# Half of the pooled features behind the attention's first scores, and products of the identity with itself at four changes of stage

## The chip, the cores and the metric

The kernel runs on one core of a Trainium2 chip. The time of a run is the device time of that core in microseconds (us), from the start of the program to its end. A core has five engines with a queue of instructions each, worked off in order and tied to one another by semaphores: TensorE (PE in the rows, its weight loads PEld), VectorE (DVE), ScalarE (ACT), GpSimd (POOL) and SyncE (SP), which here issues most DMA transfers. TensorE's results go to PSUM banks, which VectorE or ScalarE must read before the next product of that bank.

## The reference, cut to what matters

Two blocks on 256 rows of 1024 features, in float32. The first block is one layer with three groups of dilated window attention and a pooling branch; the second is two layers with modulated LayerNorms, a mixer (scans in layer 0, window attention in layer 1) and a squared-ReLU MLP of width 4096. Layer 0 works on the 256 latent rows and 256 context rows, layer 1 needs of the context only keys and values.

```python
# first block
h = rmsnorm(x, norm_g[l]) * (1.0 + scale) + shift
qkv, z_attn, u_pool, z_pool, g_attn, g_pool = split(h @ w_in[l])
# per group: o = softmax(q k^T + bias) v over a dilated band; merged over groups by log-sum-exp
y_attn = (attn * silu(z_attn)) @ w_attn_br[l]
pooled = multiscale_pool(u_pool)            # trailing means over 2, 4, 8, 16 rows, minus the row
y_pool = ((pooled @ pool_w[l]) * pool_scale[l] * silu(z_pool)) @ w_pool_br[l]
x = x + gate * ((sigmoid(g_attn) * y_attn + sigmoid(g_pool) * y_pool) @ w_out[l])
# second block, layer i (xc: the context's rows)
h = x * (1 + sc1) + sh1;  hc = xc * (1 + csc1) + csh1
y = mixer(h, hc) @ w_out                    # i = 1: window attention over latent and context keys
x = layer_norm(alpha * x + g1 * y)
x = layer_norm(alpha * x + g2 * (square(relu((x * (1 + sc2) + sh2) @ w1)) @ w2))
# i = 0: the same two residual steps for xc
```

## The kernel before, in words

**Products.** Every large product is made of three TensorE matmuls of fp32r operands (`mm3`, lines 159 to 161): each operand is split into a rounded high part and a remainder, and hi·hi, hi·lo and lo·hi are added up in one PSUM bank. Weights arrive by DMA in tiles of 512 KB (`raw`), and ScalarE (line 135, `whi`) and VectorE (line 136, `wlo`) split them. `gemm_a` puts features on the partitions, `gemm_b` rows. The banks of products have the name `mm`; `S` holds scores, `T` transposes, `O` smaller results.

**Order.** The program is written as one Python program, and a scheduler puts its instructions on each engine in an order that it works out along a timeline of its own. `tc.issue_after(x)` forces what is issued in its scope behind the instruction x. `queued[...]` keeps the last instruction of a kind. On the chip each engine then keeps that order: an instruction that waits holds back all that stand behind it on its engine.

**First block.** After q, k, v and `z_attn` the 512 pooled features `u` are computed by two `gemm_a` of 256 features, 48 matmuls each (lines 583 and 584); GpSimd forms their trailing sums and VectorE subtracts (lines 587 to 598). The attention follows (function `attention`): for each half of the heads and each tile of 128 queries, scores on TensorE (line 630), softmax on VectorE and ScalarE (line 642), transposes of the result (`pr`, and `xs`, via line 195), products with v (line 654). Between these, `fill(n)` takes steps from a list of fillers, which form the conditioning vectors of the second block: DMA of a tile of `w_mod` (`mvraw`), its products with the condition on TensorE (line 245, two matmuls of 512 columns for each tile), and sums on VectorE (line 288). Behind the first softmax stands `fill(3)`.

**Second block.** `modulate` takes one tile of 128 normalised rows (T = 0 and 1 are the context's, 2 and 3 the latent's): two groups of four transposes into a bank `T` (line 195), ScalarE scales and shifts each 128x128 square (line 342, `hf`), VectorE splits the result into high part and remainder (lines 345 and 346, `hBh`, `hBl` in layer 0's MLP, `hCh`, `hCl` for layer 1's projection, `hDh`, `hDl` for layer 1's MLP; `hBh0b` and the like are second halves). What precedes it for a tile is a LayerNorm: two `bn_stats` (line 360), aggregation, an inverse square root on GpSimd (line 200) and the normalising pass on VectorE (line 374).

- Layer 0's MLP begins with the products of `up(0)` (banks `os_`).
- The keys and values of layer 1 begin at `kb_`: the loop takes the latent half first (`half` = 1: keys by `col_part`, values by `gemm_b`, then `modulate` of context tile T = 1 and the queries of the first pair of heads), then the context half. At the end of layer 0 the tiles are normalised in the order 2, 3, 0, 1; in the program text the `modulate` of tile 0 is the last ahead of `kb_`, and that of tile 1 stands in the loop. The latent half needs only tiles 2 and 3.
- `window(kv, c, qt)` makes the scores of the window attention (line 1289), from `Q`, half of which is moved to other partitions by a DMA (`qr`), and from `KK`.
- Layer 1's MLP begins with `up(0)` in its own form: for i = 0 and 1 a `gemm_b` of 24 matmuls on latent tile 2 + i, ReLU and square on ScalarE (lines 1067 and 1068), four transposes of `f`, and a split.

Of the kernel before, what the change touches and what calls it, by code (L numbers as in the profile page):

```python
# [10 lines left out]
F32 = mybir.dt.float32  # L11
# [84 lines left out]
def body(tc, a, cst, out):  # L96
    nc = tc.nc
    with ExitStack() as ctx:
# [7 lines left out]
        def bank(tag):  # L106
            return psum.tile([P, 512], F32, tag=tag, name=tag, bufs={"mm": 3, "S": 2, "T": 2, "O": 1}[tag])
# [49 lines left out]
        def mm3(o, lhs, rhs, first, last):  # L157
            (lh, ll), (rh, rl) = lhs, rhs
            nc.tensor.matmul(o, lh, rh, start=first, stop=False)  # L159
            nc.tensor.matmul(o, lh, rl, start=False, stop=False)  # L160
            queued["mm"] = nc.tensor.matmul(o, ll, rh, start=False, stop=last).ins  # L161

        def col_part(o, ws, j, xs_):

# [11 lines left out]
        def gemm_b(ws, xh, xl, t):  # L176

            n = ws[0][0].shape[-1]
            o = bank("mm")[:, :n]
            for k, w in enumerate(ws):  # L180
                mm3(o, (xh[:, k, t * P:(t + 1) * P], xl[:, k, t * P:(t + 1) * P]), w, k == 0, k == len(ws) - 1)
            return o
# [10 lines left out]

        def transpose(o, i, n=P):
            return nc.tensor.transpose(o, i, ident[:n, :n])  # L195

        def rsqrt(v, n):

# [131 lines left out]
            nc.vector.tensor_add(B, B, sh[:, :, vec])  # L330
            return A, B

        def modulate(z, cols, dst, t0):

            A, B = cols
            for c in range(0, KC, 4):
                pt = bank("T")
                hf = tmp([P, 4, P], "hf")
                for i in range(4):
                    transpose(pt[:, i * P:(i + 1) * P], z[:, (c + i) * P:(c + i + 1) * P])  # L340
                for i in range(4):
                    queued["hf"] = nc.scalar.activation(hf[:, i, :], pt[:, i * P:(i + 1) * P], AF.Identity, scale=A[:, c + i:c + i + 1],  # L342
                                                        bias=B[:, c + i:c + i + 1]).ins
                hi, lo = (t[:, c:c + 4, t0:t0 + P] for t in dst)
                nc.vector.tensor_copy(hi, hf)
                queued["mod"] = nc.vector.tensor_sub(lo, hf, hi.bitcast(F32)).ins  # L346
# [232 lines left out]
        for i in range(2):  # L579
            silu2(za[:, 2 * i:2 * i + 2, :], gemm_a(w_in, 4608 + 256 * i, xk))  # L580


        for i in range(2):
            nc.scalar.copy(u[:, 2 * i:2 * i + 2, :], gemm_a(w_in, 5120 + 256 * i, xk))
        nc.gpsimd.dma_start(pw, a["pool_w"][0].rearrange("g c e -> c g e"))
        nc.gpsimd.dma_start(icnt, cst["icnt"])
        prev = u
        for s in range(4):
            w_ = 1 << s
            cur = wsum if s == 3 else p1t.tile([P, 4, S], F32, tag="sq", name="wtmp")  # L590
            nc.gpsimd.tensor_add(cur[:, s:, w_:], prev[:, s:, w_:], prev[:, s:, :S - w_])
            nc.gpsimd.tensor_copy(cur[:, s:, :w_], prev[:, s:, :w_])
            if s < 3:
                nc.gpsimd.tensor_copy(wsum[:, s, :], cur[:, s, :])
            prev = cur
        nc.gpsimd.tensor_mul(wsum[:, :, 0:16], wsum[:, :, 0:16], icnt)
        for g in range(4):
            nc.vector.scalar_tensor_tensor(wsum[:, g, :], wsum[:, g, :], 0.5 ** (g + 1), u[:, g, :], op0=ALU.mult, op1=ALU.subtract)

        spare = xs.rearrange("p t n -> p (t n)")  # L600
        yab = slot("h0b", "yab", [P, 2, 4, S], F32R)
# [3 lines left out]
            fill(1)  # L605
        fillers.append(quadcols("b", 2 * D, rows="b0"))
        fillers.append(quadcols("sc2", 4 * D, D // 4))

        def attention(h2):
            Bs = []  # L610
# [5 lines left out]
            for qt in range(2):  # L616
# [8 lines left out]
                for g0, g1 in parts:  # L625
# [5 lines left out]
                    for e in range(2):  # L631
# [1 line left out]
                        nc.vector.tensor_tensor_reduce(out=prs[e][:, g0:g1, 0:nk], in0=sv[e], in1=Bs[e][:, g0:g1, 256 - nk:256], scale=-1.0,  # L633
                                                       scalar=3.0e38 if mins[e] is None else mins[e], op0=ALU.add, op1=ALU.min, accum_out=m)
                        mins[e] = m
                fill(3)
                for e in range(2):
                    pv = prs[e][:, :, 0:nk]
                    den = small.tile([P, 1], F32, tag="den", name="den")
# [411 lines left out]
        def mlp(layer, Ts, xks, y, pool, mid, late, norm, after):  # L1051
# [4 lines left out]
            def up(g):  # L1056

                if g == 3:
                    rate[0] = 3
                fx = (main, pool)[g % 2].tile([P, 8, n], F32R, tag=("qkb", "fx")[g % 2], name="fx")  # L1060
                fh, fl = fx[:, 0:4], fx[:, 4:8]
                if layer and g < 1:
                    ws = w_b(w1, 512 * g)
                    for i in range(2):
                        o = gemm_b(ws, *h2, i)
                        f = pool.tile([P, 512], F32, tag="f", name="f", bufs=2)
                        nc.scalar.activation(f, o, AF.Relu)
                        nc.scalar.activation(f, f, AF.Square)
                        pt = bank("T")
                        for c in range(4):  # L1070
                            transpose(pt[:, c * P:c * P + P], f[:, c * P:c * P + P])
                        tv = pt.rearrange("p (c n) -> p c n", c=4)
                        split(fh[:, :, i * P:i * P + P], fl[:, :, i * P:i * P + P], tv)
                os_ = [bank("mm" if i < 2 else "S")[:, :n] for i in range(4)] if not layer and g == 0 else None
                if not layer and g == 0:
                    ws = [w_a(w1, 256 * i) for i in range(2)]
                    for part, xk_ in xks[0]:
                        for i in range(2):
                            for j in range(2):
                                col_part(os_[2 * i + j][:, part], ws[i], j, xk_)  # L1080
                            mid()
                for i in range(0 if layer and g < 1 else 2):
                    if g:
                        ws = w_a(w1, 512 * g + 256 * i)
                    for j in range(2):
                        if g:
                            o = bank("mm")[:, :n]
                            col_part(o, ws, j, xks[1])
                        else:
                            o = os_[2 * i + j]  # L1090
                        f = pool.tile([P, n], F32, tag="f", name="f", bufs=2)
                        nc.scalar.activation(f, o, AF.Relu)  # L1092
                        nc.scalar.activation(f, f, AF.Square)
                        split(fh[:, 2 * i + j, :], fl[:, 2 * i + j, :], f)
                with tc.issue_after(queued["split"]):
                    late(g)
                if g == 0:
                    rate[0] = 2
                return fh, fl
# [63 lines left out]
        cc = mod_cols("c0b", 2, 6, m0["sc2"], m0["b"][:, 8:16], 1)  # L1163
        cx = mod_cols("x0b", 2, 6, m0["sc2"], m0["b"][:, 8:16], 0)
        h1 = new_h("hB")
        mod0 = lambda T: modulate(r0[:, T, :], (cc, cx)[T // 2], h1, P * T)
        proj_out(r0, a["ev_w_out_2"][0], yH, yL, range(4), mod0)
        lg.close()

# [89 lines left out]
        kT = gc.rearrange("p (j n) -> p j n", j=2)  # L1259
        vN = p4.tile([P, 4, 256], F32, tag="vN", name="vN")  # L1260
        wk, wv = w_a(wq, 1024), w_a(wq, 1280)
        kb_ = [bank("mm"), bank("mm")]
        KK = slot("A0", "KK", [P, 2, 2, 2, 512], F32R)
        for half, xk_ in ((1, hx), (0, hc)):
            hs = slice(S * half, S * half + S)
# [17 lines left out]
        def window(kv, c, qt):  # L1283

            qs = slice(P * qt, P * qt + P)
            sp = [bank("S"), bank("S")]
            for e in range(2):
                for part in range(2):
                    queued["qk"] = nc.tensor.matmul(sp[e], Q2[:, kv % 2, e, c % 2, qs], KK[:, part, kv // 2, kv % 2, :], start=part == 0, stop=part == 1).ins  # L1289
# [109 lines left out]
```

## Time and profile before

| | |
|---|---|
| three runs | 1313.48, 1318.32 and 1324.63 us, median 1318.32 us |
| profiled execution | 1323.18 us, of which the span of the engines' work 1321.4 us |
| TensorE busy | 1272.4 us, 96% of the span, 7777 instructions |
| VectorE, ScalarE, GpSimd busy | 869.6 us (66%), 590.6 us (45%), 85.6 us (6%) |
| mean granted TensorE clock | 0.981 of full speed |
| DMA | 223.80 MB, mean 169 GB/s |

In the rows further down each instruction or group is written as start, duration (us), engine, line, operation, output and inputs, stationary and moving shape for matmuls, and a count; a bracket tells how long the engine had stood idle before it and what ended that. TensorE overlaps neighbouring matmuls, so a matmul's price is the distance from its start to the next one's start and not its duration. The granted clock is 1.00 at 2.4 GHz and 0.50 at 1.2 GHz. A float32 matmul (not fp32r) leaves two records.

### The profile page before, as it was taken

The page shows a single profiled execution, that of the slowest core. Times are in us where ns is not written, and L with a number is a line of the kernel's source. Part 1 is how long each engine was busy: PE and PEld are TensorE (multiplying, and loading weights), DVE is VectorE, ACT ScalarE, POOL GpSimd, SP SyncE. Part 2 cuts the span into 40 slices and gives each one's busy share as a digit, 9 for nine tenths or more (in the row PEclk, how much of TensorE's full clock was granted, in tenths as well). Part 3 has the DMA queues.
Part 4 walks back from the last instruction along what each step waited for, and adds up shares of the span by engine and source line. Part 5 has one row for each costly group of instructions (what it writes and reads, how often), then busy time and mean ns, then how long its engine had stood idle before and what let it go on. Part 6 is the DMA issues. An engine that isn't in the chain of part 4 may idle for free. (4 is left out here: it accounts for less than half of the span.)

```text
span 1321.4 us, 19813 instructions
## 1 busy us (share of the span) xinstructions
PE 1272.4 (96%) x7777; PEld 1045.9 (79%) x7777; DVE 869.6 (66%) x1344; ACT 590.6 (45%) x957; POOL 85.6 (6%) x148
## 2 busy tenths in 40 slices
PE   6999999999999999998999999999998899999996
PEld 5889845998887777778777777777888776788894
DVE  3568844696643357675868876677597677566567
ACT  4434534445431453326334333323445796655660
POOL 2010031000102100001010000000010000000000
PEclk9999969999999999998999999999999999999998
DMA  9789877675441412325656556664345214465651
GB/s 326 263 299 346 271 221 228 206 235 160 148 127 31 127 40 65 128 67 168 201 174 204 163 190 207 207 207 160 96 137 163 71 55 155 150 190 180 187 178 46
DMA packets 140964, 223.80 MB, mean 169 GB/s; under 512 B 8748, under 2 KB 88796, under 8 KB 140870
## 3 DMA queue, kind: packets, MB, share of 16 engines
q1 hardware_dynamic: 134832, 207.64, 49.2%
q0 software_dynamic: 5296, 14.33, 3.6%
q8 instruction: 61, 1.00, 0.3%
q10 hardware_dynamic: 742, 0.55, 0.1%
q14 instruction: 33, 0.27, 0.1%
HBM read 218.23 MB, written 1.12 MB: 166 GB/s over the span
## 5 line engine op out<-in xcount | busy, mean ns | idle before, releaser
L135 ACT CAST whi<-raw 128x1024 fp32r<-128x1024 f32 x261 | 272.9, 1051 | 372.8 <-PE mm L161 203.5
L136 DVE TENSOR_TENSOR wlo<-raw,whi 128x1024 fp32r<-128x1024 f32 x261 | 317.4, 1222 | 162.4 <-ACT whi L135 160.0
L159 PE MATMUL mm<-whi,fx 128*128 128x512 f32 x384 | 153.2, 399 | 2.6 <-DVE y L1112 1.2
L160 PE MATMUL mm<-wlo,fx 128*128 128x512 f32 x384 | 151.4, 395 | 0.0
L161 PE MATMUL mm<-whi,fx 128*128 128x512 f32 x384 | 147.4, 396 | 0.0
L288 DVE SCALAR_TENSOR_TENSOR mva<-mvraw,cst_m,mva 128x1024 f32<-128x1024 f32 x98 | 123.3, 1280 | 0.2
L160 PE MATMUL mm<-A1a,whi 128*128 128x256 f32 x352 | 99.8, 284 | 0.0
L159 PE MATMUL mm<-A1a,whi 128*128 128x256 f32 x352 | 99.8, 283 | 0.0
L161 PE MATMUL mm<-A1a,wlo 128*128 128x256 f32 x352 | 99.6, 283 | 0.0
L160 PE MATMUL mm<-hBl,whi 128*128 128x512 f32 (+1 forms) x256 | 98.4, 384 | 0.1
L159 PEld LDWEIGHTS mm<-whi,fx 128*128 128x128 f32 x384 | 72.2, 188 | 25.1 <-DVE y L1112 6.0
L161 PEld LDWEIGHTS mm<-whi,fx 128*128 128x128 f32 x384 | 72.2, 188 | 17.6 <-DVE fx L111 0.4
L160 PEld LDWEIGHTS mm<-wlo,fx 128*128 128x128 f32 x384 | 72.3, 188 | 16.0
L160 PEld LDWEIGHTS mm<-A1a,whi 128*128 128x128 f32 x352 | 66.2, 188 | 2.4 <-issue 2.3
L111 DVE TENSOR_TENSOR fx<-f,fx 128x512 fp32r<-128x512 f32 (+1 forms) x60 | 34.0, 566 | 51.5 <-ACT fx L110 51.3
L159 PEld LDWEIGHTS mm<-A1a,whi 128*128 128x128 f32 x352 | 66.4, 189 | 1.2 <-issue 1.0
L161 PEld LDWEIGHTS mm<-A1a,wlo 128*128 128x128 f32 x352 | 66.3, 188 | 0.8 <-issue 0.8
L1112 DVE TENSOR_TENSOR y<-y,mm 128x512 f32<-128x512 f32 x72 | 47.1, 683 | 28.2 <-PE mm L161 28.1
L160 PE MATMUL mm<-hDl,whi 128*128 128x256 f32 x224 | 63.1, 282 | 0.0
L1092 ACT ACTIVATE f<-mm 128x512 f32<-128x512 f32 (+1 forms) x58 | 28.4, 490 | 73.0 <-PE mm L161 73.0
L160 PEld LDWEIGHTS mm<-hBl,whi 128*128 128x128 f32 x256 | 48.8, 191 | 10.7 <-DVE hBl L346 0.4
L159 PE MATMUL mm<-whi,hA 128*128 128x512 f32 x128 | 51.2, 401 | 0.0
(519 smaller groups left out, 2846.2 us busy)
## 6 DMA issues: line engine op xcount, KB each, us to landing
raw<-in_mlp_w_dram SPq DMA_DIRECT2D x128, 512.0 KB, 4.1
mvraw<-in_w_mod_dram SPq DMA_DIRECT2D x96, 512.0 KB, 4.7
raw<-in_w_in_dram SPq DMA_DIRECT2D x64, 512.0 KB, 5.4
raw<-in_ev_w_in_dram SPq DMA_DIRECT2D x25, 512.0 KB, 3.9
raw<-in_od_w_qkv_dram SPq DMA_DIRECT2D x12, 512.0 KB, 3.5
mvraw<-in_w_ada_dram SPq DMA_DIRECT2D x10, 512.0 KB, 6.4
raw<-in_w_out_dram SPq DMA_DIRECT2D x8, 512.0 KB, 4.7
raw<-in_ev_w_out_dram SPq DMA_DIRECT2D x8, 512.0 KB, 4.4
```

The source lines that it names most:

```text
L111: queued["split"] = nc.vector.tensor_sub(lo, src, hi.bitcast(F32)).ins
L135: nc.scalar.copy(hi, raw)
L136: queued["lo"] = nc.vector.tensor_sub(lo, raw, hi.bitcast(F32)).ins
L159: nc.tensor.matmul(o, lh, rh, start=first, stop=False)
L160: nc.tensor.matmul(o, lh, rl, start=False, stop=False)
L161: queued["mm"] = nc.tensor.matmul(o, ll, rh, start=False, stop=last).ins
L288: nc.vector.scalar_tensor_tensor(acc, raw, stat[:, k, m:m + 1], acc, op0=ALU.mult, op1=ALU.add)
L1092: nc.scalar.activation(f, o, AF.Relu)
L1112: nc.vector.tensor_add(y[:, T, hs], y[:, T, hs], o)
```

## The change

Two things are changed.

1. In the first block only the first 256 pooled features are computed ahead of the attention. For the other 256 the weights are loaded and split there (`wu`), but the 48 matmuls, the copy to `u` and the whole pooling stand in a new function `pooling`, which is called behind the first softmax of the attention, in place of the `fill(3)` there. That call's three filler steps come later.
2. A helper `awake(n, o, behind)` issues n float32 matmuls of the 128x128 identity with itself into the bank o, forced behind an instruction. Nobody reads these results; the bank's own first product overwrites them. There are 28: 6 and 3 in `modulate` of tile 2 for layer 0's MLP (ahead of each group of four transposes), 2 at layer 0's `up(0)`, 5 at `kb_`, 8 ahead of the first window scores, and 4 at layer 1's `up(0)`. The 2, the 5 and the 4 go through a list `ahead`, and `mm_bank` issues them into the next `mm` bank that is taken, behind `queued["last"]`: the last matmul of a product, or the last transpose of a `modulate`, whichever the program text has put there last.

```diff
-            queued["mm"] = nc.tensor.matmul(o, ll, rh, start=False, stop=last).ins
+            queued["mm"] = queued["last"] = nc.tensor.matmul(o, ll, rh, start=False, stop=last).ins
...
+        ahead = []
+        def awake(n, o, behind):
+            with tc.issue_after(behind):
+                for _ in range(n):
+                    w = nc.tensor.matmul(o[:, :P], ident, ident, start=True, stop=True).ins
+            return w
+        def mm_bank():
+            o = bank("mm")
+            if ahead:
+                awake(ahead.pop(0), o, queued["last"])
+            return o
...
-        def modulate(z, cols, dst, t0):
+        def modulate(z, cols, dst, t0, keep=(0, 0)):
...
+                if keep[c // 4]:
+                    with tc.issue_after(queued["T"]):
+                        queued["awake"] = awake(keep[c // 4], bank("S"), queued["last"])
                 for i in range(4):
-                    transpose(pt[:, i * P:(i + 1) * P], z[:, (c + i) * P:(c + i + 1) * P])
+                    with tc.issue_after(queued["awake"]) if keep[c // 4] else nullcontext():
+                        queued["T"] = queued["last"] = transpose(pt[:, i * P:(i + 1) * P], z[:, (c + i) * P:(c + i + 1) * P]).ins
...
-        for i in range(2):
-            nc.scalar.copy(u[:, 2 * i:2 * i + 2, :], gemm_a(w_in, 5120 + 256 * i, xk))
-        nc.gpsimd.dma_start(pw, a["pool_w"][0].rearrange("g c e -> c g e"))
...
+        nc.scalar.copy(u[:, 0:2, :], gemm_a(w_in, 5120, xk))
+        wu = w_a(w_in, 5376)
...
+        def pooling():
+            o = bank("mm").rearrange("p (j n) -> p j n", j=2)
+            for j in range(2):
+                col_part(o[:, j, :], wu, j, xk)
+            nc.scalar.copy(u[:, 2:4, :], o)
+            nc.gpsimd.dma_start(pw, a["pool_w"][0].rearrange("g c e -> c g e"))
...
-                fill(3)
+                if (h2, qt) == (0, 0):
+                    pooling()
+                else:
+                    fill(3)
...
                 if layer and g < 1:
+                    ahead.append(4)
                     ws = w_b(w1, 512 * g)
...
-                os_ = [bank("mm" if i < 2 else "S")[:, :n] for i in range(4)] if not layer and g == 0 else None
+                if not layer and g == 0:
+                    ahead.append(2)
+                    os_ = [(mm_bank() if i < 2 else bank("S"))[:, :n] for i in range(4)]
...
-        mod0 = lambda T: modulate(r0[:, T, :], (cc, cx)[T // 2], h1, P * T)
+        mod0 = lambda T: modulate(r0[:, T, :], (cc, cx)[T // 2], h1, P * T, (6, 3) if T == 2 else (0, 0))
...
-        kb_ = [bank("mm"), bank("mm")]
+        ahead.append(5)
+        kb_ = [mm_bank(), mm_bank()]
...
+            if (kv, c, qt) == (0, 0, 0):
+                awake(8, sp[0], queued["last"])
```

The scheduler puts the program in order again, so instructions without a line in the diff move too. Three places follow; the line numbers of the changed kernel are up to 35 higher.

TensorE at the end of layer 0's MLP and the start of layer 1's projection, before: `fx` products are the last ones of the MLP, `y` is the tile to be transposed (the four transposes here are the second group of latent tile 3), and `hCh` products are those of the keys and values. The eight transposes of context tile 0 stand some 95 rows further on.

```order
L161 MATMUL mm<-whi,fx 128x512
L195 MATMUL T<-ident,y_5688 128x128 x4
L159 MATMUL mm<-hCh_8358,whi 128x256 x2
L159 MATMUL mm<-whi,hCh_8358 128x256
L160 MATMUL mm<-wlo,hCh_8358 128x256
```

The same place in the changed kernel:

```order
L161 MATMUL mm<-whi,fx 128x512
L195 MATMUL T<-ident,y_5699 128x128 x12
L203 MATMUL mm<-ident 128x128 x5
L159 MATMUL mm<-hCh_8371,whi 128x256
L160 MATMUL mm<-hCl,whi 128x256
```

The twelve transposes are the four from before and the eight of context tile 0, which now stand ahead of every product of the keys and values, with the five products of the identity (line 203) between.

TensorE at the start of layer 1's MLP, before: `aHL` products are the last of the output projection, `r` is the tile to be transposed, `hDh` products are those of `up(0)`. Behind these rows stand 24 such products in all, and then the eight transposes of latent tile 3.

```order
L195 MATMUL T<-ident,r_9841 128x128 x8
L159 MATMUL mm<-whi,aHL 128x512
L160 MATMUL mm<-wlo,aHL 128x512
L161 MATMUL mm<-whi,aHL 128x512 x2
L159 MATMUL mm<-whi,hDh_9847 128x512
L160 MATMUL mm<-wlo,hDh_9847 128x512
L161 MATMUL mm<-whi,hDl 128x512
```

The same place in the changed kernel:

```order
L195 MATMUL T<-ident,r_9867 128x128 x8
L159 MATMUL mm<-whi,aHL 128x512
L160 MATMUL mm<-wlo,aHL 128x512
L161 MATMUL mm<-whi,aHL 128x512 x2
L195 MATMUL T<-ident,r_9867 128x128 x8
L203 MATMUL mm<-ident 128x128 x4
L159 MATMUL mm<-whi,hDh_9873 128x512
L160 MATMUL mm<-wlo,hDh_9873 128x512
```

The eight transposes of tile 3 have moved ahead of the products of tile 2, with the four products of the identity; 48 `hDh` and `hDl` products follow without a break.

TensorE at the start of the attention, before: the 48 products of the second half of `u` come first, then scores (`S`), eight filler products (line 245), scores of the next tile and the first softmax's transposes.

```order
L630 MATMUL S<-h1a 128x128 x3
L630 MATMUL S<-h0a 128x128 x2
L245 MATMUL O<-mvraw,cst_m 32x512 x8
L630 MATMUL S<-h1a 128x256 x4
L195 MATMUL T<-ident,xs 128x128 x3
L195 MATMUL T<-ident,pr 128x128 x3
L630 MATMUL S<-h0a 128x256 x2
L245 MATMUL O<-mvraw,cst_m 32x512 x2
```

In the changed kernel the six rows of scores of the first tile stand ahead of the 48 products (left out here, all of the form of line 159), and the transposes ahead of the eight filler products:

```order
L656 MATMUL S<-h1a 128x128 x4
L656 MATMUL S<-h0a 128x128 x2
L195 MATMUL O<-ident,mvb 128x128 x2
L195 MATMUL T<-ident,xs 128x128 x3
L195 MATMUL T<-ident,pr 128x128 x3
L260 MATMUL O<-mvraw,cst_m 32x512 x8
L656 MATMUL S<-h0a 128x256 x2
L260 MATMUL O<-mvraw,cst_m 32x512 x2
```

At layer 0's MLP the order of TensorE is that of before, with 6, 3 and 2 products of the identity ahead of the transposes and products that used to follow a wait. On VectorE the order from the last MLP products of layer 0 to the normalising pass of tile 0, and from the last output products of layer 1 to that of tile 3, is that of before.

## Rows read from the trace of the kernel before

**Rows 1.** The page's first part: busy time, share of the span and instructions.

```profile
PE 1272.4 (96%) x7777; PEld 1045.9 (79%) x7777; DVE 869.6 (66%) x1344; ACT 590.6 (45%) x957; POOL 85.6 (6%) x148
```

**Rows 2.** Table by stretch: length, busy PE, PEld, DVE, ACT, POOL, clock, DMA.

```profile
172.80:193.40 20.60, 20.60 (x61) 8.70 (x59) 6.44 (x22) 4.25 (x10) 3.24 (x7) 0.50 0.58 171
599.70:606.30 6.60, 5.35 (x22) 4.66 (x23) 6.14 (x14) 3.15 (x10) 1.27 (x1) 0.50 1.02 380
...
606.30:620.00 13.70, 13.70 (x118) 13.70 (x118) 2.65 (x5) 7.10 (x13) 0.00 (x0) 1.00 0.17 61
...
976.00:1018.00 42.00, 37.34 (x306) 36.09 (x305) 32.60 (x56) 24.68 (x46) 1.44 (x2) 1.00 0.51 151
1018.00:1023.00 5.00, 5.00 (x26) 4.82 (x26) 4.27 (x10) 1.89 (x6) 0.00 (x0) 0.66 0.44 131
...
1018.00:1107.00 89.00, 84.18 (x600) 65.74 (x601) 65.76 (x166) 68.85 (x171) 0.00 (x0) 0.96 0.21 64
...
1118.20:1121.70 3.50, 3.50 (x10) 2.72 (x9) 3.50 (x5) 0.63 (x1) 0.00 (x0) 0.52 1.01 368
```

**Rows 3.** TensorE in order of time, eight float32 matmuls of 128 columns and their follower.

```profile
409.46 1.95 PE L835 MATMUL T<-yg,vx 128*128 128x128 f32 x16
411.16 0.47 PE L159 MATMUL mm<-whi,hA 128*128 128x512 f32 x1
```

**Rows 4.** TensorE in order of time, start of the attention.

```profile
162.26 0.48 PE L630 MATMUL S<-h1a 64*128 64x128 f32 x2
...
167.54 0.55 PE L195 MATMUL T<-ident,xs 128*128 128x128 f32 x3 [0.63 <-DVE xs L642]
...
171.79 1.05 PE L245 MATMUL O<-mvraw,cst_m 128*32 128x512 f32 x4 [1.62 <-DMA mvraw<-in_w_mod_dram]
```

**Rows 5.** TensorE in order of time, start of layer 0's MLP.

```profile
598.72 0.66 PE L195 MATMUL T<-ident,r 128*128 128x128 f32 x4 [2.22 <-ACT hf L342]
600.11 1.12 PE L195 MATMUL T<-ident,r 128*128 128x128 f32 x4 [0.74 <-ACT hf L342]
601.95 0.79 PE L159 MATMUL mm<-hBh,whi 128*128 128x256 f32 x2 [0.72 <-DVE hBh L345]
...
603.89 0.41 PE L159 MATMUL mm<-hBh,whi 128*128 128x256 f32 x1
604.10 0.41 PE L160 MATMUL mm<-hBl,whi 128*128 128x256 f32 x1
```

**Rows 6.** TensorE in order of time, from layer 0's MLP to the window attention.

```profile
975.44 0.60 PE L195 MATMUL T<-ident,y 128*128 128x128 f32 x4
975.84 0.38 PE L159 MATMUL mm<-hCh,whi 128*128 128x256 f32 x1
...
988.32 1.04 PE L195 MATMUL T<-ident,y 128*128 128x128 f32 x8
...
1017.99 1.16 PE L1289 MATMUL S<-KK,Q 128*128 128x512 f32 x4 [2.06 <-DMA Q<-qr]
```

**Rows 7.** VectorE in order of time, the normalising pass of context tile 0.

```profile
985.48 0.81 DVE L374 TENSOR_SCALAR y<-y,mvst,rs_y 128x1024 f32<-128x1024 f32 x1 [0.54 <-POOL rs_y L200]
```

**Rows 8.** TensorE in order of time, start of layer 1's MLP.

```profile
1114.34 0.64 PE L161 MATMUL mm<-whi,aHL 128*128 128x512 f32 x2
1115.85 0.50 PE L159 MATMUL mm<-whi,hDh 128*128 128x512 f32 x1 [0.88 <-DVE hDh L345]
...
1124.59 1.09 PE L195 MATMUL T<-ident,r 128*128 128x128 f32 x8
1127.34 0.66 PE L195 MATMUL T<-ident,f 128*128 128x128 f32 x4 [1.66 <-ACT hf L342]
...
1135.31 0.39 PE L159 MATMUL mm<-whi,fx 128*128 128x512 f32 x1
...
1139.37 0.50 PE L159 MATMUL mm<-whi,fx 128*128 128x512 f32 x1 [0.67 <-ACT fx L110]
```

**Rows 9.** VectorE in order of time, the normalising pass of latent tile 3.

```profile
1123.72 0.81 DVE L374 TENSOR_SCALAR r<-r,mvst,rs_y 128x1024 f32<-128x1024 f32 x1 [0.68 <-POOL rs_y L200]
```

More of the change, by code (lines that the diff above doesn't have):

```diff
@@ L178, in gemm_b @@
             n = ws[0][0].shape[-1]
-            o = bank("mm")[:, :n]
+            o = mm_bank()[:, :n]
             for k, w in enumerate(ws):
@@ L580, in body @@
             silu2(za[:, 2 * i:2 * i + 2, :], gemm_a(w_in, 4608 + 256 * i, xk))
-        for i in range(2):
-            nc.scalar.copy(u[:, 2 * i:2 * i + 2, :], gemm_a(w_in, 5120 + 256 * i, xk))
-        nc.gpsimd.dma_start(pw, a["pool_w"][0].rearrange("g c e -> c g e"))
[L586 to L598, printed above, removed]
+        nc.scalar.copy(u[:, 0:2, :], gemm_a(w_in, 5120, xk))
+        wu = w_a(w_in, 5376)
         spare = xs.rearrange("p t n -> p (t n)")
@@ L607, in body @@
         fillers.append(quadcols("sc2", 4 * D, D // 4))
+        def pooling():
[4 more added lines that the diff above has]
+            nc.gpsimd.dma_start(pw, a["pool_w"][0].rearrange("g c e -> c g e"))
+            nc.gpsimd.dma_start(icnt, cst["icnt"])
+            prev = u
+            for s in range(4):
+                w_ = 1 << s
+                cur = wsum if s == 3 else p1t.tile([P, 4, S], F32, tag="sq", name="wtmp")
+                nc.gpsimd.tensor_add(cur[:, s:, w_:], prev[:, s:, w_:], prev[:, s:, :S - w_])
+                nc.gpsimd.tensor_copy(cur[:, s:, :w_], prev[:, s:, :w_])
+                if s < 3:
+                    nc.gpsimd.tensor_copy(wsum[:, s, :], cur[:, s, :])
+                prev = cur
+            nc.gpsimd.tensor_mul(wsum[:, :, 0:16], wsum[:, :, 0:16], icnt)
+            for g in range(4):
+                nc.vector.scalar_tensor_tensor(wsum[:, g, :], wsum[:, g, :], 0.5 ** (g + 1), u[:, g, :], op0=ALU.mult, op1=ALU.subtract)
         def attention(h2):
```

## Prediction

> **What bounds the kernel now.** The page's busy line comes first: TensorE is busy 96% of the span [rows 1], so what TensorE loses is lost, and what the other engines save is worth nothing unless TensorE waits for them. Second, the table by stretch shows where its clock stood at half, 1.2 GHz: 20.6 us at the start of the attention, 6.6 at the start of layer 0's MLP, most of the first 3.5 or so of the window attention, and 3.5 in layer 1's MLP [rows 2]. Third, TensorE in order of time at each of these places shows what came ahead: idle stretches of 0.6 to 2.2 us, with a releaser [rows 4, 5, 6, 8]. The change goes for these two things, waits and the slow clock behind them. So each of its six places is costed by the wait it fills, what it puts on the path, and what it moves.
>
> **The price of an identity product.** No instruction of before is one, but eight float32 matmuls of the same shape take from 409.46 to 411.16 us at full clock [rows 3]: 1.70 / 8 = 0.213 us each, and by the two levels of the clock 0.425 at half. For comparison, a fp32r product of 256 columns takes 13.70 / 118 = 0.116 us at full clock [rows 2] and 604.10 - 603.89 = 0.21 at half [rows 5]; one of 512 columns takes double, 0.23. All 28 cost 6.0 us at full clock if nothing hides them; hidden behind waits they cost nothing.
>
> **Layer 0's MLP: 6, 3 and 2 products.** They take 1.28, 0.64 and 0.43 us, and stand ahead of waits of 2.22, 0.74 and 0.72 us that end by ScalarE's and VectorE's work, not TensorE's [rows 5]. Their cover is those waits; without it they cost 2.3. If the clock holds, 3.0 us of records between 603.3 and 606.3 at 0.21 fall to 0.116: a gain of 1.4. Bounds: 0 (the clock falls all the same) to 2.5 (the second transposes, 1.12 us at half clock, run full too). I take **-1.4**.
>
> **Attention: half of the pooled features moved.** Before, the first scores start at 162.26, behind the 48 products; the first transposes of the softmax wait 0.63 us at 167.54, and at 171.79 a filler product has waited 1.62 us for its DMA; then the clock is at half until 193.4 [rows 2, 4]. In the changed order the scores stand ahead of the 48 products (48 x 0.116 = 5.6 us), which is more than the 5.3 us from first scores to first transposes, so that wait of 0.63 goes. But the eight filler products now stand behind the transposes, about 1.5 us later than before. The DMA that 171.79 waits for goes into the buffer that the first of these sets free, so it is issued about as much later, and TensorE reaches its product with little else to do. I expect a wait of at least the same size there and a half clock after it, as before. What is left is the 0.63 us, and that three filler steps leave a stretch at half clock for a later one at full clock (about 1 us for each two filler products [rows 4], twice that at half), minus the later DMA. I take **-2**; bounds +2 (DMA late, steps crowd a later stage) and -10 (clock holds: half of 20.6).
>
> **Layer 1's keys and values: 5 products, and what they drag along.** This is the place that decides. `mm_bank` ties them behind `queued["last"]`, and in the program text that is the last transpose of context tile 0. So the transposes of tile 0 now stand ahead of the first product of the latent half, which doesn't need them. Before, TensorE finished tile 3's transposes and went from 975.84 through the products of the latent half while VectorE normalised tile 0 [rows 6]. That pass runs from 985.48 to 986.29 [rows 7], behind a VectorE queue whose order is unchanged and holds nothing made by those products. So the transposes can't start before 986.3, and what stands behind them on TensorE is the whole projection.
>
> The Trainium skill ("TensorE: Matmul & The Clock Gate", Part 2, step on LDWEIGHTS) says that TensorE may pull weight loads ahead but that the matmuls themselves stay in program order; by that rule nothing slips past the waiting transposes and the hole is whole, as the sum below has it; without it the products could run as before and the third rival would hold. No row of before shows a matmul that overtakes another.
>
> The hole is 986.3 - 975.9 = 10.4 us. After it the clock is surely low for a while, as after holes of 2 us before [rows 2, 5]: eight transposes 1.0 us at full clock [rows 6], about 1.7 at half; five identity products 2.1 at half. Then the rest until the first window scores: 288 products x 0.118 = 34.0, of which none was made; eight transposes of tile 1, 0.9; eight identity products, 1.7; and 0.5 to 2.5 us of waits for ScalarE behind tile 1's transposes (before, 42.0 us of span hold 34.0 + 1.7 of such work, so 6.3 of waits [rows 2], of which 2.06 is the DMA of `Q` [rows 6] and others belong to tile 0's chain, which now has its time ahead): I take 0.5. Sum: 986.3 + 1.7 + 2.1 + 34.0 + 0.9 + 1.7 + 0.5 = 1027 against 1017.99, so +9. The DMA of `Q` no longer ends anything there, because more products lie behind the queries' product than before, so the eight identity products have no wait to fill and cost their 1.7. Given back: no half clock behind the first scores (0.34 of 5 us [rows 2], 1.7 us), and something in the window attention, since VectorE and ScalarE split its weights during the hole: TensorE idles 89.0 - 84.2 = 4.8 us in it [rows 2], of which I take 1.5. Net **+6**; bounds +3 and +11 (nothing given back, 2 more of waits).
>
> **Layer 1's MLP: 4 products, same trap.** The last transpose in the program text is tile 3's, so these eight stand ahead of `up(0)` of tile 2. Before, TensorE did tile 2's 24 products from 1115.85 (half clock among them [rows 2]) while VectorE normalised tile 3 until 1124.53 [rows 8, 9]. Now TensorE idles from 1115.0 to 1124.6. Then: transposes 1.7 at half, identity products 1.7 at half, 48 products x 0.233 = 11.2: 1139.2. Before, those 48 products were done at 1135.31, and 12 of the next kind and the transposes of `f` by 1139.37 [rows 8]. Still to do at 1139.2 are eight transposes (1.0), the ReLU, square and split chain of the second `f` (about 1.5 us of wait that used to be covered), and the 12 products (2.8): 1144 to 1144.5, so **+4.5**; bounds +2 (clock back soon, chain covered) and +7.
>
> **Sum.** -1.4 - 2 + 6 + 4.5 = +7.1 us against the profiled 1323.18: 1330.3. That execution lies 4.9 us above the median of the runs, so I name 1318.32 + 7.1, about 1326 us.
>
> **Rivals.**
> - *The holes cost all they show* (slower): nothing is given back in the window attention, the clock stays low longer behind each hole, and the identity products stay on the path. Layer 1's two places then cost 11 + 7 and the others give 2: +16, 1334 us. For it speaks that TensorE is the bound at 96% [rows 1]; against it, that the window attention does have 4.8 us of waits.
> - *The clock holds in the attention* (faster side): if TensorE meets no wait from the scores to 171.79, the 20.6 us at half clock shrink by up to 10 and the 0.63 goes; with the rest of the sum, -10 - 1.4 + 6 + 4.5 = -1: 1317 us. It turns to faster by over 1% only if the two holes are under 4 us together too. It is decided at one place: the filler product at 171.79 must find its tile landed. For it: more scores stand ahead of that product now than before. Against it: its DMA starts later.
> - *The order's holes are filled* (faster): the normalising passes of tile 0 and tile 3 end earlier than in the trace, so that transposes wait for little. Then all identity products fill waits, and -1.4 - 2 - 1.7 (window start) - 1.7 (layer 1's half clock, half of 3.5) = about -7: 1312 us. It decides if the passes end before 977 and 1116; against it is that VectorE is busy nearly without a break up to them, with unchanged order [rows 7, 9].
> - *A rule that would change the sum*: that the identity products do not keep the clock up. Then layer 0's -1.4 is 0 and the sum is +8.5: 1327 us.
>
> **How the numbers follow.** My forecast with its own spread (1320 to 1331): 0.50. The holes at full cost: 0.24. Clock holding in the attention: 0.14. Holes filled: 0.06. Identity products without effect on the clock: 0.06. The range 1312 to 1336 leaves out about 2 in 10. A measurement here tells apart about 1%, 13.2 us: below 1305.1 lies only a sum of the second and third rival, 0.07; above 1331.5 most of the first and the forecast's upper end, 0.27; between, 0.66.
>
> **What would show it.** In the profile after: TensorE idle ahead of the transposes of `y` at about 976 to 986 and of `r` at about 1115 to 1125, released by VectorE's line for the normalising pass; the first window scores some 9 us later than before, measured from the end of layer 0; no wait for `Q`; the clock at full speed at the start of layer 0's MLP; a wait for `mvraw` at the start of the attention with half clock behind it. I am wrong if the first two idle stretches are short, or if the attention runs at full clock.

## The result and the profile after

The changed kernel takes 1326.22 us (median of 11 runs, 1323.44 to 1328.64); the kernel before, run beside it, 1318.21 us (11 runs). The ratio is 1.0065, 95% interval 1.0046 to 1.0084: slower by two thirds of a per cent. That lies inside the 1% below which the prediction expected a measurement to tell nothing apart, but the interval leaves out 1, so it is beyond noise. The profiled execution has a span of 1323.8 us.

The page's busy line and the granted clock in 40 slices, changed kernel (to be set against [rows 1]); in the second line each digit is the clock of one slice in tenths of full speed, 9 for 90% or more:

```profile
PE 1264.3 (96%) x7833; PEld 1046.6 (79%) x7833; DVE 868.9 (66%) x1344; ACT 590.4 (45%) x957; POOL 86.2 (7%) x148
PEclk9999989999999999999999999999989998999998
```

TensorE has 56 records more, two for each of the 28 identity products, and is still busy less: 1264.3 us against 1272.4, since less of its work ran at half clock. The span grew all the same. The list of TensorE's waits names the two places:

```profile
PE T L195 <- DVE y L393: 10.4, 1, 10.4
PE T L195 <- DVE r L393: 9.7, 1, 9.7
```

Engine, what it waited to start and for what, us in total, times, longest. The first is the transposes of context tile 0, the second those of latent tile 3, both waiting for the normalising pass.

TensorE in order of time at layer 1's keys, changed kernel, where [rows 6] stood before:

```profile
964.72 0.60 PE L195 MATMUL T<-ident,y 128*128 128x128 f32 x4
...
975.72 1.94 PE L195 MATMUL T<-ident,y 128*128 128x128 f32 x8 [10.39 <-DVE y L393]
977.45 2.34 PE L203 MATMUL mm<-ident 128*128 128x128 f32 x10
979.45 0.56 PE L159 MATMUL mm<-hCh,whi 128*128 128x256 f32 x1
...
1015.18 1.95 PE L203 MATMUL S<-ident 128*128 128x128 f32 x16
1016.89 1.17 PE L1324 MATMUL S<-KK,Q 128*128 128x512 f32 x4
```

Between tile 3's last transposes and the first product of the keys lie 14.7 us; before the change it was 0.4. The first window scores no longer wait for `Q`. VectorE's row that ends the wait (now both context tiles in one row, where [rows 7] had one):

```profile
974.76 1.70 DVE L393 TENSOR_SCALAR y<-y,mvst,rs_y 128x1024 f32<-128x1024 f32 x2 [0.54 <-POOL rs_y L215]
```

TensorE in order of time at layer 1's MLP, changed kernel, answering to [rows 8]:

```profile
1121.29 1.94 PE L195 MATMUL T<-ident,r 128*128 128x128 f32 x8 [9.70 <-DVE r L393]
1123.03 1.60 PE L203 MATMUL mm<-ident 128*128 128x128 f32 x8
1124.38 0.48 PE L159 MATMUL mm<-whi,hDh 128*128 128x512 f32 x1
...
1135.61 0.60 PE L195 MATMUL T<-ident,f 128*128 128x128 f32 x4
1137.87 0.50 PE L159 MATMUL mm<-whi,fx 128*128 128x512 f32 x1 [1.67 <-ACT fx L110]
...
1141.67 0.39 PE L159 MATMUL mm<-whi,fx 128*128 128x512 f32 x1
```

The same at layer 0's MLP, answering to [rows 5]:

```profile
587.08 1.50 PE L203 MATMUL S<-ident 128*128 128x128 f32 x12
589.46 0.66 PE L195 MATMUL T<-ident,r 128*128 128x128 f32 x4 [0.88 <-ACT hf L361]
589.95 0.83 PE L203 MATMUL S<-ident 128*128 128x128 f32 x6
590.86 0.66 PE L195 MATMUL T<-ident,r 128*128 128x128 f32 x4
591.35 0.61 PE L203 MATMUL mm<-ident 128*128 128x128 f32 x4
592.69 0.51 PE L159 MATMUL mm<-hBh,whi 128*128 128x256 f32 x2 [0.73 <-DVE hBh L364]
```

Here the products of the identity fill 1.3 of 2.2 us and all of the 0.74, and the clock holds. They cost nothing on the path: from the first of these transposes to the second group and on to the first product of `hBh` it takes 1.40 and 1.83 us, before the change 1.39 and 1.84 [rows 5].

In the attention, answering to [rows 4], the wait of the first softmax's transposes is gone and that for the filler's tile is still there. A new wait of 0.58 us has come up between them: scores that wait for VectorE's first pass of the softmax (`m`, line 659):

```profile
164.48 0.55 PE L195 MATMUL T<-ident,xs 128*128 128x128 f32 x3
...
166.70 1.92 PE L260 MATMUL O<-mvraw,cst_m 128*32 128x512 f32 x16
...
169.83 0.78 PE L656 MATMUL S<-h1a 64*128 64x128 f32 x5 [0.58 <-DVE m L659]
...
172.29 1.92 PE L260 MATMUL O<-mvraw,cst_m 128*32 128x512 f32 x4 [1.12 <-DMA mvraw<-in_w_mod_dram]
```

The table by stretch of the changed kernel, for [rows 2]; the third figure from the end of a row is the granted clock:

```profile
172.00:178.80 6.80, 6.51 (x21) 2.37 (x22) 2.61 (x7) 0.95 (x4) 3.28 (x6) 0.51 1.00 351
586.00:593.00 7.00, 5.32 (x42) 4.66 (x41) 6.71 (x11) 7.00 (x18) 1.52 (x3) 1.00 0.95 302
970.70:980.90 10.20, 5.18 (x25) 5.21 (x26) 7.30 (x16) 2.90 (x8) 1.44 (x2) 0.51 0.17 51
1114.00:1124.30 10.30, 3.01 (x15) 3.04 (x16) 6.75 (x12) 2.93 (x7) 0.56 (x1) 0.51 0.73 258
```

The clock is at half in the attention for 6.8 us instead of 20.6, full at layer 0's MLP, and at half for 10 us each at the two new idle stretches.

### The profile page after: what moved, and what is told of

The parts are those of the page before. It is cut to its first block, busy times and chain, and to the rows that moved or that the text cites. A ratio compares the mean times of both kernels' runs of the same rounds, so it can differ in the third digit from the quotient of the medians.

```text
span 1323.8 us, 19919 instructions
## 1 busy us (share of the span) xinstructions
PE 1264.3 (96%) x7833; PEld 1046.6 (79%) x7833; DVE 868.9 (66%) x1344; ACT 590.4 (45%) x957; POOL 86.2 (7%) x148
## 3 DMA queue, kind: packets, MB, share of 16 engines
HBM read 218.23 MB, written 1.12 MB: 166 GB/s over the span
## 4 chain that ended last, share of the span: by engine, by line
PE 66%; DVE 6%; issue 1%; ACT 0%; POOL 0%; DVEq 0%
PE mm L159 19%; PE mm L160 19%; PE mm L161 19%; PE T L195 2%; PE O L1351 1%; DVE wlo L136 1%; PE S L1324 1%; PE T L864 1%; DVE y L1144 0%; PE S L852 0%; DVE st L379 0%; PE O L309 0%; PE S L160 0%; PE S L968 0%; PE S L161 0%
```

## The experiments

All ratios are to the kernel before on the same chip; the changed kernel's is 1.0065. The runs of the experiments stand on three chips, so kernels are best compared by their ratios; a difference of two ratios has an uncertainty of some 4 us. First, whose fault the two idle stretches are: the order or the identity products.

**Both ties mended.** The five and the four products are tied behind the last product instead of the last transpose; the two of layer 0's MLP keep their tie:

```diff
-                awake(ahead.pop(0), o, queued["last"])
+                n, kind = ahead.pop(0)
+                awake(n, o, queued[kind])
...
-                    ahead.append(4)
+                    ahead.append((4, "mm"))
...
-        ahead.append(5)
+        ahead.append((5, "mm"))
```

> All of the change, but the five identity products at layer 1's keys and the four at its MLP are tied behind the last product instead of the last transpose, so the transposes of tile 0 and of tile 3 stand behind the products again, as before the change. Theory 'order' (the two idle stretches of 10.4 and 9.7 us are the loss, and the order makes them): both stretches vanish from the profile, and of the 9.6 and 5.7 us that the two stages lost at least 12 come back, less the 2.3 that the window attention gained: about 1315 us, ratio to before about 0.997. Rival 'products' (the identity products on the path cost the time, the idle stretches are given back elsewhere): 1322 to 1326 us.

Measured: 1309.54 us, ratio 0.9935 (0.9912 to 0.9958). TensorE at the same two places:

```profile
964.34 1.28 PE L203 MATMUL mm<-ident 128*128 128x128 f32 x10
965.45 0.60 PE L195 MATMUL T<-ident,y 128*128 128x128 f32 x4
965.81 0.36 PE L159 MATMUL mm<-hCh,whi 128*128 128x256 f32 x1
...
1102.41 1.05 PE L203 MATMUL mm<-ident 128*128 128x128 f32 x8
1103.46 0.50 PE L159 MATMUL mm<-whi,hDh 128*128 128x512 f32 x1
...
1112.59 1.09 PE L195 MATMUL T<-ident,r 128*128 128x128 f32 x8 [1.47 <-DVE r L394]
```

The keys' products start 0.4 us behind the transposes, and tile 3's transposes wait 1.47 us and not 9.7. The whole of it came back, 16.7 us by the medians and 17 by the ratios, more than the 12 expected, and the kernel is faster than both the changed one and the one before. The theory that the order makes the loss holds.

**Order alone.** The nine products are left out; the first products of the keys and of the MLP are tied behind the same transposes:

```diff
-        ahead.append(5)
-        kb_ = [mm_bank(), mm_bank()]
+        tie = queued["last"]
+        kb_ = [mm_bank(), mm_bank()]
...
-                col_part(kb_[j][:, hs], wk, j, xk_)
+                with tc.issue_after(tie) if half and not j else nullcontext():
+                    col_part(kb_[j][:, hs], wk, j, xk_)
```

(and likewise around the first `gemm_b` of layer 1's MLP)

> The nine identity products at these two places are left out, but the first products of the keys and of layer 1's MLP are tied behind the same transposes as in the change. Theory 'order': the two idle stretches stay at about 10 us each and the time is that of the change less 2 to 4 us: 1322 to 1325 us. Rival 'products': the time falls to about 1315 us.

Measured: 1324.38 us, ratio 1.0052 (1.0028 to 1.0076). Its waits are those of the change to the tenth:

```profile
PE T L195 <- DVE y L393: 10.4, 1, 10.4
PE T L195 <- DVE r L393: 9.7, 1, 9.7
```

Against the changed kernel that is 1.8 us less by the medians and 1.7 by the ratios, which is not clear of noise; nine products at half clock would take 3.6 us (9 at 0.40 us). The rival, that they are the main cost, falls.

**Nine products dropped, with their ties.** The two `ahead.append` of the five and the four are removed, nothing else.

> All of the change without the five and the four identity products, and so without their ties. Theory 'order': about 1314 us, one below the run with mended ties, since nine products at 0.21 us are 1.9 us of which some fill waits. Rival 'clock' (the identity products keep the clock up at these two places and are worth their time): 3 us or more above the run with mended ties, with half clock at the window attention's or the MLP's start.

Measured: 1309.70 us, ratio 0.9940 (0.9918 to 0.9962), the same as with mended ties and not the 1 us less that was expected. At these two places identity products are neither worth nor cost anything that can be measured, if they do not order anything.

**One tie mended at a time.** The edit of the first experiment, at the keys alone and at the MLP alone, so that the other place keeps its idle stretch.

> The change with the mended tie at layer 1's keys alone; the four products of the MLP stay tied behind tile 3's transposes. The prediction gave the MLP's place +4.5 us (2 to 7); set against the second profile of the kernel before it measures +7.7. So against the 1309.5 us with both ties mended: 1314 if the prediction's size holds, 1317 if that of the second pair of profiles does.

> The change with the mended tie at layer 1's MLP alone; the five products of the keys stay tied behind tile 0's transposes. The prediction gave this place +6 us net, after what the window attention gives back; the pairs of profiles say 9.5 less 1.7 to 2.3. So against the 1309.5 us with both ties mended: 1315.5 by the prediction, 1317 by the profiles; 1319 or more if nothing is given back.

Measured: 1317.18 us, ratio 1.0014 (0.9998 to 1.0030), with the keys mended, and 1318.57 us, ratio 1.0031 (1.0013 to 1.0048), with the MLP mended. The first meets the expectation from the second pair of profiles, 1317; the second lies between 1317 and the 1319 of nothing given back. Against 1309.54 us the MLP's stretch alone is worth 7.6 us and the keys' 9.0, and the two sum to the 16.7 of both. But these two runs stand on another chip than the one with both mended. By the ratios, each to the kernel before on its own chip (median 1315.18 us here, 1316.35 there), they are 10 and 13 us with some 4 us of uncertainty each, and their sum of 23 is more than the 17 of both; how well the two add up is not settled closer than that. Either way the MLP's place costs more than the 4.5 us of the prediction.

Second, the attention.

**Pooled features alone.** The move, and no identity product anywhere.

> Only the pooled features' second half is moved, no identity product anywhere. My prediction had -2 us for it (-10 to +2): about 1316 us. The pair of profiles shows the attention 9.3 us shorter, nearly all of it by a half-clock stretch of 6.8 instead of 20.5 us: if that is what the move does every time, 1309 us; if the long stretch was particular to that one execution of the kernel before, 1314 to 1317 us.

Measured: 1311.99 us, ratio 0.9952 (0.9929 to 0.9974): 4.4 us by the medians, 6.3 by the ratio. It lies between the two expectations, and the gain is larger than the 2 us of the prediction.

**Pooled features alone, fillers kept.**

```diff
                 if (h2, qt) == (0, 0):
                     pooling()
-                else:
-                    fill(3)
+                fill(3)
```

> Only the pooled features moved, no identity product, and the three filler steps stay behind the first softmax in addition. Theory 'scores ahead': the gain comes from the softmax having 48 products beside it, so this kernel is like the one with the features moved alone, 1312 us within 2. Rival 'fewer fillers': the gain comes from the three steps having left a stretch that waits for its DMAs, so this kernel falls back to 1314 to 1316 us.

Measured: 1311.34 us, ratio 0.9961 (0.9942 to 0.9979), no different within some 4 us. So the three filler steps that left the place have no part in the gain that these runs can resolve. Of the two theories that leaves 'scores ahead', which no run tests by itself.

**The kernel before, once more.**

> The kernel before, unchanged, profiled a second time. Theory 'one execution': the 20.5 us at half clock in the attention were particular to the profiled execution, whose mean clock of 0.981 lies at the low end; this profile then shows a shorter stretch there and a span some 5 to 8 us shorter, ratio 1.00. Rival 'every time': the stretch is about 20 us again.

Measured: 1316.78 us, ratio 1.0018 (0.9988 to 1.0047), span of the profiled execution 1315.2 us, 6.2 shorter, as the theory 'one execution' had it. The two waits in the attention that answer to [rows 4], and the table by stretch, in this second execution:

```profile
166.87 0.55 PE L195 MATMUL T<-ident,xs 128*128 128x128 f32 x3 [0.64 <-DVE xs L642]
...
170.39 1.05 PE L245 MATMUL O<-mvraw,cst_m 128*32 128x512 f32 x4 [0.89 <-DMA mvraw<-in_w_mod_dram]
```

```profile
162.00:172.00 10.00, 8.24 (x58) 4.05 (x59) 8.12 (x21) 5.31 (x12) 8.13 (x12) 1.00 0.82 277
172.00:193.00 21.00, 20.44 (x118) 9.66 (x115) 11.41 (x39) 8.49 (x21) 4.62 (x8) 1.00 0.95 265
213.70:220.50 6.80, 6.80 (x35) 3.63 (x36) 1.98 (x6) 1.51 (x3) 0.00 (x0) 0.51 0.68 216
596.00:602.80 6.80, 5.96 (x25) 5.27 (x26) 6.08 (x13) 2.68 (x8) 1.27 (x1) 0.51 1.02 394
1112.00:1132.00 20.00, 16.49 (x75) 12.36 (x74) 15.17 (x22) 12.94 (x21) 1.09 (x2) 1.00 0.55 190
```

The stretch behind 172, at half clock for 20.6 us in [rows 2], is at full clock here, and so is layer 1's MLP, half for 3.5 us in [rows 2]; the attention was at half clock for 6.8 us at another place. Of the four stretches of [rows 2] only that of layer 0's MLP is at the same place in both; the window attention has 6.8 us in each, but from 1019.4 and 1036.4 in the first (3.4 each) and from 1029.3 in the second. 34 runs of the kernel before, on the chip of both ties mended, order alone, nine products dropped and pooled features alone, go from 1309.58 us at a mean clock of 0.991 to 1326.90 at 0.980. The profile on which the prediction was made, at 0.981, came from the long end.

**Identity products alone.** All 28 with the ties of the change, the pooled features as before.

> All 28 identity products with their ties as in the change, the pooled features as before. If the parts add up, the change's 1.0065 less the 0.9952 of the moved features alone gives about 1.011, some 1329 us; the half clock in the attention is as often there as in the kernel before. If the moved features are worth what the pair of profiles showed (9 us), 1333 us or more.

Measured: 1331.71 us, ratio 1.0117 (1.0094 to 1.0140), from four runs. The parts add up: 1.0117 times the 0.9952 of the move is 1.0068, against 1.0065.

**Further identity products, for the window attention's wait.** Both ties mended, and nine more products ahead of the transposes of the second window's softmax, which wait 2.0 us for its denominators:

```diff
                 tp = bank("T")
+                if (kv, c, qt, e) == (0, 0, 1, 0):
+                    awake(9, tp, queued["qk"])
```

> The change with mended ties, and nine more identity products in the window attention ahead of the transposes that wait 2.0 us for the softmax's denominators, where every profile so far shows 3.4 us at half clock. If they hold the clock: that stretch is gone and 1.7 us with it, about 1308 us against 1309.5. If they only delay the third window's scores: 1310 to 1312 us.

Measured: 1311.97 us, ratio 0.9970 (0.9955 to 0.9985), against 0.9935 without. The wait with both ties mended, and then TensorE at the place with the nine products:

```profile
1023.36 1.94 PE L195 MATMUL T<-ident,pr 128*128 128x128 f32 x8 [2.03 <-DVE den L1338]
```

```profile
1016.96 2.27 PE L203 MATMUL T<-ident 128*128 128x128 f32 x18
1019.17 1.09 PE L1354 MATMUL O<-PT,vN 128*64 128x128 f32 x14
1020.18 1.20 PE L1325 MATMUL S<-KK,Q 128*128 128x512 f32 x4
...
1023.17 0.66 PE L195 MATMUL T<-ident,pr 128*128 128x128 f32 x4 [0.67 <-DVE pr L1344]
```

The clock did hold there; in the eleven other profiles the window attention has 3.4 or 6.8 us at half clock. But the scheduler put the products ahead of products with v and scores that were ready or nearly due, and not into the wait. They take 2.2 us there, and from the first window scores to the first transposes of `r` it takes 93.7 us, against 91.8 with both ties mended: more than the clock gave back.

## Why the prediction was right, and where its terms were not

The total was forecast at 1326 us (+7.1 over the kernel before, by its median) and measured 1326.22 (+8.0). (1318.32 + 7.1 is 1325.4, which the prediction rounds to about 1326.) By its steps it was less right than that. The start of the same instructions in both profiles of the kernel before and in that of the changed one, in us:

| start of | before | before, second profile | changed | stage's difference to the second (to the first) | predicted |
|---|---|---|---|---|---|
| first transposes of `r`, layer 0 | 590.38 | 586.21 | 581.13 | -5.1 (-9.3) | -2 |
| first transposes of `y` | 969.47 | 965.42 | 958.76 | -1.6 (-1.5) | -1.4 |
| first window scores | 1017.99 | 1014.05 | 1016.89 | +9.5 (+9.6) | +9 |
| first transposes of `r`, layer 1 | 1112.53 | 1108.02 | 1109.15 | -1.7 (-2.3) | -3 |
| 13th `fx` product, layer 1 | 1139.37 | 1132.80 | 1141.67 | +7.7 (+5.7) | +4.5 |
| last product | 1307.84 | 1301.65 | 1310.12 | -0.4 (0.0) | 0 |

The differences are of each stage alone, the row's shift less that of the row above. Their sum against the second profile is +8.4, like the medians; against the first it is +2.3, since that execution was a long one.

- **Layer 1's keys: right in every step up to the first window scores.** The idle stretch was put at 10.4 us and is 10.39; eight transposes at half clock 1.7, measured 977.45 - 975.72 = 1.73; five identity products 2.1, measured 979.45 - 977.45 = 2.00; the eight ahead of the scores 1.7 on the path, measured 1016.89 - 1015.18 = 1.71; from there the products. The diff does not say that the transposes would move; the two orders side by side do, and VectorE's unchanged order gives the length. The Trainium skill ("TensorE: Matmul & The Clock Gate", Part 2, step on LDWEIGHTS) says that matmuls stay in program order. This trace agrees: not one product of the latent half started in the 10.39 us, though before the change they ran while the same normalising pass was going on. What the window attention would give back was put too high, 3 us for 1.7 to 2.3. Of its two parts the clock came as sized: 3.4 us at half clock, from 1032.0, where the profile before had 6.8. The 1.5 us for weights split during the idle stretch came hardly or not at all.
- **Layer 1's MLP: mechanism right, size too small, and outside its bounds of 2 to 7 against the second profile.** The term was made from two ends. That of the changed kernel is 32.5 us from the first transposes to the 13th `fx` product, where the prediction's 1144.0 to 1144.5 make 31.5 to 32, and its +4.5 makes 31.3. That of before was taken as 26.8 us, from a profile with half clock in this stage: 3.5 us in [rows 2], and 3.4 more from 1128.6 that the prediction did not list. The second profile has none, and 24.8 us. The table by stretch, of the first profile and of the second:

```profile
1112.53:1139.37 26.84, 22.55 (x92) 16.91 (x90) 17.86 (x28) 16.95 (x30) 1.43 (x3) 0.87 0.61 215
```

```profile
1108.02:1132.80 24.78, 19.71 (x91) 14.47 (x89) 17.66 (x28) 16.87 (x30) 1.43 (x3) 1.00 0.63 219
```

  So the step that failed is the base: clock that one execution lost there was counted as part of the kernel. That is 2.1 of the 3.2 us that were missed; the rest is at the changed kernel's end.
- **Attention: a gain, but larger than the 2 us put down, and its cause is open.** The wait of 0.63 us went, as forecast, but one of 0.58 us for the softmax's first pass came up a little later, in all nine profiles with the features moved. The wait for the filler's tile stayed; it was forecast to be at least as long as before and is 1.12 us here, 1.04 to 2.81 in the nine. "A half clock after it, as before" failed in its size: 6.8 us here and none in four of the nine. The table sets all twelve profiles side by side. The fifth column is the stretch from a product of `mva` with `sel` ahead of the attention (at 114.3 to 116.1 us) to the first transposes of `r`, which holds the same TensorE work in all of them (2977 or 2978 records):

| profile | features | wait for the filler's tile | half clock in the attention | stretch to `r` | half clock at layer 0's MLP |
|---|---|---|---|---|---|
| before | old place | 1.62 | 20.5 | 475.4 | 6.8 |
| before, once more | old place | 0.89 (1.88 later) | 6.8 | 471.9 | 6.8 |
| identity products alone | old place | 1.15 | 6.8 | 469.7 | none |
| changed | moved | 1.12 | 6.8 | 465.9 | none |
| keys' tie mended | moved | 1.65 | 3.4 | 464.9 | none |
| MLP's tie mended | moved | 2.81 | 3.4 | 466.4 | none |
| fillers kept | moved | 1.34 | 3.4 | 463.9 | 6.8 |
| window attention's wait | moved | 1.52 | 3.4 | 464.5 | none |
| order alone | moved | 1.40 | none | 465.7 | none |
| nine dropped | moved | 1.09 | none | 463.6 | none |
| both ties mended | moved | 1.04 | none | 465.7 | none |
| pooled features alone | moved | 1.20 | none | 464.4 | 6.8 |

  The clock is the cause of a part at most. With the features moved, the four profiles without half clock are no shorter than the four with 3.4 us: where the clock held, TensorE waited more for the fillers' tiles (2.1 to 3.3 us in all in those four, 1.1 to 2.8 in the other five). And at the same 6.8 us of half clock the old place takes 471.9 and 469.7 us against 465.9, of which 1.7 us are a further 3.4 us of half clock near 541 that those two executions had. So some 2 to 4 us came without the clock, as far as single executions tell. Which of the waits or overlaps gives them, and why the clock holds more often, no run took apart. What was said of the three filler steps is not borne out: the run that keeps them is no slower, within some 4 us.
- **Layer 0's MLP: right.** The profiles of the kernels without the 6, 3 and 2 products (four) all have 6.8 us at half clock there, those with them (eight) none. That also answers the rival by which these products do not keep the clock up.
- **The rivals, and luck.** Two rivals were each partly true. "The holes cost all they show" had 18 us for layer 1's two places and the sum 10.5; measured are 9.5 - 1.7 + 7.7 = 15.5. "The clock holds in the attention" had -10 and the sum -2; measured is -5.1, though not by the clock alone. That the two errors, 3 us too little gain in the attention and 3 us too little loss in the MLP, have opposite signs is why the total came out to within a microsecond. It is luck, and no merit of the working.

## What to carry to other kernels

When a helper ties work behind "the last instruction of a kind", ask which instruction that is in the order in which the engine can run it, not in the order of the text: here the last transpose in the text was the one whose input came last, and tying ahead of the products dragged 10 us of waiting in front of work that was ready. Fill work that was tied to what runs just before the wait cost nothing that could be measured here, and tied to what ends the wait it cost the wait. Before a stretch of low clock in a profile is priced as part of a kernel, look at a second execution, or at the spread of the mean clock over its runs, and ask what TensorE would wait for there at full clock.

## What the runs showed of the hardware

- The clock does not fall at the same places in every execution of one program. The kernel before had half clock for 20.5 us behind waits of 0.63 and 1.62 us in one execution, and none at the same place, behind waits of 0.64 and 0.89 us, in another. Over 34 runs that is a range of 17 us, with the mean clock following the time from 0.991 to 0.980.
- Eleven identity products in waits of 2.2, 0.7 and 0.7 us held the clock at 2.4 GHz in eight profiles of eight, where four of four without them fell to 1.2 GHz. Behind an idle stretch that had brought the clock down, the products ran at half clock themselves (0.40 us each at the keys); without them the time was 1.8 us less, which is not clear of noise.
- Half clock cost little where TensorE also waits for DMAs: in the attention with the features moved, four executions with the attention at full clock took 463.6 to 465.7 us for a stretch in which four with 3.4 us of it at half clock took 463.9 to 466.4, with waits for tiles in place of the slow clock.
